# A 20-space weight ring of 8 KiB spaces becomes one of 16 KiB spaces: gate and up of an expert in one transfer

## The chip, the cores and the metric

The kernel runs on 1 core of one Trainium2 chip. The metric is the device time of one execution in microseconds (us); lower is better. Before the change it is 892.16 us, the median of three runs (891.83 to 892.23).

The program feeds the engines by DMAs that SyncE issues: each has 128 rows, one for each partition of the on-chip memory, and the profile counts one packet for each row, and one of a few bytes for each of the 16 DMA engines when a transfer ends.

## What is computed

One decoder block over 256 tokens of width 1024, in float32: a projection of x, dilated attention and a gated linear recurrence side by side, their merge and a layer norm, then a mixture of experts, and a last layer norm. The part that the change touches is the mixture:

```python
s = sigmoid(h @ w_router)                      # 256 tokens, 64 experts
idx, g = top 8 experts of a token, out of its best 4 groups; g normalised, times 2.5
for each expert e and the tokens routed to it:
    a = silu(xb @ w_gate[e]) * (xb @ w_up[e])  # 1024 -> 256
    out = (a @ w_down[e]) * g                  # 256 -> 1024, added to the tokens
y_moe = sum of those + shared_expert(h)
x = layer_norm(alpha * x1 + y_moe + sigmoid(x1 @ ple_gate) * (p @ ple_proj))
```

Each expert has 3 MiB of weights: gate and up with 2 MiB, down with 1 MiB; all 64 are read, 192 MiB.

## The kernel before

**The ring.** Nearly all weights pass through spaces of [128, 2048] float32, that is 8 KiB in each partition and 1 MiB in all. `slot()` (line 71) hands them out in turn from the deque `free`: it takes the first entry, puts it behind the last, and asks the pool of that entry for a tile. The pools are `ring_a` with 9 spaces from the start (line 92), `ring_b` with 6 after the attention and recurrence buffers are closed (line 434), the two spaces of `xhi` and `xlo` (line 478), the one of `x1` (line 875), and two of `ring_c` (line 1020): 18 spaces up to the third unit of experts, then 20. A load into a space waits on SyncE until every reader of its former tile is done, and SyncE issues its loads one after the other, so a waiting load holds up all behind it. Loads with `ordered` keep the order of the program. A pool hands out whichever of its spaces comes free first.

**The experts.** Experts are ranked by their number of tokens (experts 0 to 7 stand in front, `FIXED`) and done in 13 units of two passes (line 816): ten units of pairs (a pass is 2 experts of 64 token places) and three of quads (4 experts of 32 places), in the order P P Q P P P P Q P P P P Q. For a pass, `expert_weights` (line 835) takes three spaces for each expert and loads in the order: first half of gate and up of each expert (k tiles 0 to 3), second half of each (k tiles 4 to 7), down of each. The last unit loads each piece in two transfers of 512 KiB. Where rank, not number, names the expert, SyncE reads the expert's number from a register (`expert_at`).

On TensorE a pass is: `gate_up` over k tiles 0 to 3 for all its experts (`g<-raw,xe`, 3.5 us), the same over k tiles 4 to 7 (3.5 us), transposes, the down product (`g<-raw,hT`, 3.6 us), and the scatter back to the tokens (`acc`). The order of TensorE from the router on is that of the program (`PE_FIXED`).

**The third unit** (line 985, `q == LATE_AT`) is a quad unit with more in it. Its loads in order: 12 spaces of quad pass 1 (experts ranked 40 to 43), `pleg2` and `pleg3` (`late_embedding`, line 884, 1 MiB each), 12 spaces of quad pass 2 (44 to 47), `shgu0`, `shgu1` and `shd` of the shared expert (`late_shared`, line 893), one space `keep` without a load. Then the pairs ranked 8 and 9, 10 and 11, and so on follow.

**Who follows whom in the ring, before.** With 18 spaces, a load takes the space of the 18th before it. So the first halves of quad pass 1 follow the first and second halves of experts 2 and 3; its second halves follow the downs of 2 and 3 and the first halves of 4 and 5; its downs follow the second halves and downs of 4 and 5. `pleg2` and `pleg3` follow the first halves of experts 6 and 7. Quad pass 2 follows, in its order, the second halves and downs of 6 and 7, the first halves of quad pass 1, and four second halves of quad pass 1. The shared weights follow downs of quad pass 1.

Of the kernel before, what the change touches and what calls it, by code (L numbers as in the profile page):

```python
# [11 lines left out]
F32 = mybir.dt.float32  # L12
F32R = mybir.dt.float32r
# [5 lines left out]
S = 256  # L19
D = 1024  # L20
KT = D // 128
AH = 8
NE = 64
# [10 lines left out]
FIXED, SMALL, SMALL_AT = 8, 24, (2, 7, 12)  # L34
# [2 lines left out]
GS_POOL = (0, 2)  # L37
LATE_AT = 2
X_MUL, Q0 = 1, 1
X_AT, C_AT = None, (None, -1)  # L40
# [15 lines left out]
def tile_block(ctx: ExitStack, tc: tile.TileContext, a, out: bass.AP):  # L56
    nc = tc.nc
# [3 lines left out]
    const = ctx.enter_context(tc.tile_pool(name="const", bufs=1))  # L61
    free = deque()

    def add_slots(pl, n, at=None):
        for _ in range(n):
            free.insert(len(free) if at is None else at, (pl, n))

    def add_ring(n, side, name, at=None):
        add_slots(ctx.enter_context(tc.tile_pool(name=name, bufs=1, side=side, reuse_waits="tile")), n, at)

    def slot(dt=F32):

        pl, n = free[0]
        free.rotate(-1)
        return pl.tile([128, 2048], dt, name="raw", tag="raw", bufs=n)

    loads = []

    def load(dst, src, ordered=False):
        ins = nc.sync.dma_start(dst, src)  # L80
        loads.append(ins)
        if ordered:
            tc.keep_in_program_order(ins)
# [5 lines left out]
            load(t[:, c], src[:, c], ordered)  # L89
        return t  # L90

    add_ring(RING_A, "left", "ring_a")
    px0 = ctx.enter_context(tc.tile_pool(name="ringx", bufs=1))

    fixed = {"pe": False}
# [23 lines left out]
    def pieces(src, n, *engine):  # L119
# [311 lines left out]
    phg.close()  # L431
    ph.close()
    pvs.close()
    add_ring(RING_B, "right", "ring_b")


    px = ctx.enter_context(tc.tile_pool(name="px", bufs=1, side="right", reuse_waits="tile"))
# [51 lines left out]
    for i in range(2):  # L489
        for f in range(2):  # L490
            c = slice(512 * f, 512 * f + 512)
# [338 lines left out]
    def expert_at(r):  # L830

        with tc.issue_after(loads[-1].ins):
            return nc.values_load(ids[0:1, r:r + 1], engines=(mybir.EngineType.SP,), min_val=0, max_val=3 * (NE - 1))

    def expert_weights(r0, ne, last=False):

        w = [[] for _ in range(ne)]
        at = [expert_at(r0 + e) if r0 >= FIXED else None for e in range(ne)]
        for n in range(3):
            for e in range(ne):  # L840
                w[e].append(slot())
            parts = 2 if last else 1
            for part in range(parts):
                c = slice(2048 * part // parts, 2048 * (part + 1) // parts)
                for e in range(ne):
                    if at[e] is None:
                        load(w[e][n][:, c], a["exp"][3 * (r0 + e) + n][:, c])
                    else:
                        load(w[e][n][:, None, c], a["exp"][bass.ds(at[e] + n, 1)].rearrange("o p f -> p o f")[:, :, c], True)
        return w  # L850

    def gate_up(gu, kts, xe, off, w):
# [19 lines left out]
    gu0 = bank("g")  # L872
    with tc.issue_after(placed.ins):
        embed(0, gates0, emb0, x1)
    add_slots(pxx, 1, X_AT)
    into = add_emb(0, emb0, True)
    for n in range(2):
        gate_up(gu0, (2 * n, 2 * n + 1), xe, 0, w0)
# [14 lines left out]
    def late_shared():  # L893
        gu = [(raw(a["shgu"][n], ordered=True), 4) for n in range(2)]
        dn = raw(a["shd"], ordered=True)
        keep = slot(F32R)
        hs = ptg.tile([128, 2, 256], F32, name="hs", tag="tg0", bufs=2)
        hth, htl = keep[:, 0:512], keep[:, 512:1024]
        for _ in dense(gu, lambda i, ps: swiglu(hs[:, i], ps), [bank("g") for _ in range(2)]):
            pass  # L900
        hT = bank("t", (128, 2, S))
        for i in range(2):
            for ft in range(2):
                transpose(hT[:, ft, 128 * i:128 * i + 128], hs[:, i, 128 * ft:128 * ft + 128])
        hT = hT.rearrange("p f t -> p (f t)")
        act.activation(hth, hT, CP)
        dve.tensor_sub(htl, hT, hth.bitcast(F32))
        for f in range(2):
            for ft in range(2):
                n = 2 * f + ft  # L910
                whi, wlo = halves()
                act.activation(whi, dn[:, 512 * n:512 * n + 512], CP)
                dve.tensor_sub(wlo, dn[:, 512 * n:512 * n + 512], whi.bitcast(F32))
                for i in range(2):
                    c = slice(256 * ft + 128 * i, 256 * ft + 128 * i + 128)
                    for l, r in ((hth, whi), (htl, whi), (hth, wlo)):
                        mm(acc[i][f], l[:, c], r, start=False, stop=False)
# [67 lines left out]
    for q, (r0, ne) in enumerate(units):  # L985
        if q + 1 < len(units):
            nxt, xnxt, steps = unit(q + 1)
            fill = ((none, steps, steps, none),) * 2
            if q < LATE_AT:
                fill = (none, none if q else into, none if q else into, none), (none, steps, steps, steps)  # L990
            elif q == LATE_AT:
                fill = (none,) * 4, (steps,) * 4
        else:
            rows, lw = slot()[:4, :512], slot().rearrange("p (n d) -> p n d", n=2)
            for n, v in enumerate(("ln2w", "ln2b")):
                load(rows[2 * n:2 * n + 2], a[v].rearrange("(r f) -> r f", r=2), True)
            fill = (norm_weights(rows, lw),) * 4, (none,) * 4
        for pr in range(2):
            r = r0 + ne * pr
            last = q + 1 == len(units) and pr == 1  # L1000
            w = expert_weights(r, ne, q + 1 == len(units)) if r else w0

            def add(i, f, l, halves, first=not r, last=last):
                for n, r in enumerate(halves):
                    mm(acc[i][f], l, r, start=first and f == 1 and n == 0, stop=last and n == 1)
                if last:
                    dve.bn_stats(stats[:, i, f], acc[i][f])

            rest = experts(p2, bank, xe, 128 * pr, s, lambda i: gates2[:, i, r:r + ne], w, add, rest, fill[pr],
                           None if r else gu0)  # L1010
            if q == LATE_AT:
                for _ in rest:
                    pass
                rest = late_embedding() if pr == 0 else late_shared() or ()
            if q == LATE_AT and pr == 0:
                homes = deque(["tg1", "tg1", "xs", "xs", "tg0", "tg0"])
        if q == LATE_AT:
            bd.close()
            for n in range(RING_C):
                add_ring(1, "left", f"ring_c{n}", C_AT[n])  # L1020
        for _ in steps:
            pass
        s, xe = nxt, xnxt
# [42 lines left out]
    pair_no = px.tile([128, 1], F32, name="pair_no")  # L1066
    with tc.If(nr > 1):
        kept = slot()
        total = [[kept[:, 1024 * i + 512 * f:1024 * i + 512 * f + 512] for f in range(2)] for i in range(2)]
        for i in range(2):  # L1070
            for f in range(2):
# [3 lines left out]
        with tc.For_i(1, nr, 1):  # L1075
            dve.tensor_scalar(posm, posm, -float(SLOTS), None, op0=OP.add)
            dve.memset(pair_no, 0.0)
            with tc.For_i(0, NE, 2) as c0:
                with tc.tile_pool(name="po", bufs=1) as po, \
# [5 lines left out]
                    for e in range(2):  # L1085
                        w.append([])
                        at = nc.values_load(ids[0:1, bass.ds(c0 + e, 1)], engines=(mybir.EngineType.SP,),
                                            min_val=0, max_val=3 * (NE - 1))
                        for n in range(3):
                            t = slot()  # L1090
                            nc.sync.dma_start(t[:, None, :], a["exp"][bass.ds(at + n, 1)].rearrange("o p f -> p o f"))
                            w[e].append(t)
# [43 lines left out]
def constants():  # L1136
# [6 lines left out]
    c[:NE, C_COL + 1] = 3 * e  # L1143
# [13 lines left out]
def layouts(i):  # L1157
# [47 lines left out]
    e = np.empty((NE, 3, 128, 2048), np.float32)  # L1205
    gu = e[:, :2].reshape(NE, 2, 128, 4, 2, 256)
    for n, k in enumerate(("expert_w_gate", "expert_w_up")):
        gu[:, :, :, :, n] = g[k][0].reshape(NE, 2, 4, 128, 256).transpose(0, 1, 3, 2, 4)
    e[:, :2] = gu.reshape(NE, 2, 128, 2048)
    e[:, 2] = g["expert_w_down"][0].reshape(NE, 2, 128, 2, 512).transpose(0, 2, 3, 1, 4).reshape(NE, 128, 2048)  # L1210
    r["exp"] = e.reshape(NE * 3, 128, 2048)
    r.update(constants())
    return r

# [17 lines left out]
```

## Time and profile before

| | us |
|---|---|
| median of three runs | 892.16 (891.83 to 892.23) |
| the profiled execution | 890.42 |
| its span in the trace | 888.3 |
| TensorE busy in it | 853.6 (96%) |
| SyncE's DMA queue, share of 16 engines over the span | 76.3% |

Rows of the trace are in microseconds from the start of the span. In groups of instructions, `raw` is a space of the ring, `in_exp_dram` the experts' weights in HBM, `in_pleg_dram` the weights of `pleg2` and `pleg3`, `in_shd_dram` the shared expert's down weights. SPq is SyncE's sequencer, PE is TensorE's matmuls, PEld its weight loads.

### The profile page before, as it was taken

What the parts mean: (1) busy time and instruction counts of PE and PEld (TensorE: products, weight loads), DVE (VectorE), ACT (ScalarE), POOL (GpSimd) and SP (SyncE); (2) the same over time, 40 slices, a digit from 0 to 9 for tenths busy, and PEclk for the clock granted to TensorE, in tenths of its full rate; (3) what the DMA queues carried; (4) which work ended last, traced back from release to release, by engine and by line L of the source; (5) the groups of instructions that cost most, each with busy time, mean ns of one, the idle gap of its engine ahead of it and who ended that gap; (6) DMA issues with size and microseconds to landing.
All of it is one profiled execution on the core that took longest, in us unless ns stands there. A gap on an engine that the chain in (4) does not pass through costs nothing.

```text
span 888.3 us, 13995 instructions
## 1 busy us (share of the span) xinstructions
PE 853.6 (96%) x5200; PEld 563.5 (63%) x5200; DVE 380.1 (43%) x821; ACT 327.0 (37%) x650; POOL 152.0 (17%) x207
## 2 busy tenths in 40 slices
PE   8999999999999999999999989999999999999983
PEld 7899897888879999874444665454544445454220
DVE  6555555695976665773122541122221212222105
ACT  6444544567675545542112341122221212222101
POOL 1015463743300000201210000110210111020001
PEclk9999999999999999989999999999999999999997
DMA  9963424444234887447999999999999999999991
GB/s 339 420 235 127 143 96 142 148 136 144 95 124 160 347 330 308 145 156 272 380 383 401 420 420 421 420 421 421 420 422 417 421 419 422 420 421 403 410 403 63
DMA packets 43776, 270.85 MB, mean 305 GB/s; under 512 B 5252, under 2 KB 5380, under 8 KB 15544
## 3 DMA queue, kind: packets, MB, share of 16 engines
q1 hardware_dynamic: 43352, 269.20, 76.3%
q8 instruction: 42, 0.69, 0.3%
q10 hardware_dynamic: 288, 0.52, 0.2%
q0 software_dynamic: 64, 0.20, 0.1%
q14 instruction: 30, 0.25, 0.1%
HBM read 268.85 MB, written 1.05 MB: 304 GB/s over the span
## 4 chain that ended last, share of the span: by engine, by line
PE 81%; DMA 10%; DVE 6%; issue 1%; ACT 1%; SPq 1%; DVEq 0%; ACTq 0%
PE g L102 30%; PE pj L102 26%; DMA raw<-in_exp_dram 9%; PE t L102 7%; PE acc L102 5%; PE ah L102 4%; PE mix L472 2%; PE sc L102 2%; PE yp L102 1%; PE ap L379 1%; PE t L105 1%; PE pt L258 1%; DMA raw<-in_win_dram 1%; DVE hr L363 1%; PE op L102 1%
## 5 line engine op out<-in xcount | busy, mean ns | idle before, releaser
L102 PE MATMUL g<-raw,xe 128*64 128x512 f32 (+1 forms) x1024 | 196.1, 596 | 3.1 <-DMA raw<-in_exp_dram 2.3
L115 ACT ACTIVATE wh<-raw 128x512 fp32r<-128x512 f32 x213 | 132.2, 630 | 121.3 <-PE pj L102 88.3
L116 DVE TENSOR_TENSOR wl<-raw,wh 128x512 fp32r<-128x512 f32 x184 | 129.4, 715 | 91.1 <-ACT wh L115 70.5
L102 PEld LDWEIGHTS g<-raw,xe 128*64 128x64 f32 (+1 forms) x1024 | 56.8, 126 | 125.7 <-issue 109.5
L102 PE MATMUL pj<-xhi,wh 128*128 128x256 f32 x448 | 128.8, 288 | 0.2 <-DVE hq L364 0.2
L102 PE MATMUL pj<-xlo,wh 128*128 128x256 f32 x448 | 128.2, 286 | 0.0
L102 PE MATMUL pj<-xhi,wl 128*128 128x256 f32 x448 | 128.0, 286 | 0.0
L828 DVE TENSOR_TENSOR h<-h,g 128x256 f32<-128x256 f32 x52 | 21.9, 421 | 200.0 <-ACT h L826 199.1
L790 POOL TENSOR_SCALAR sel<-cst,posm 128x64 fp32r<-128x64 f32 (+1 forms) x120 | 46.4, 419 | 342.3 <-PE t L102 332.1
L102 PE MATMUL g<-raw,hT 128*64 128x512 f32 (+1 forms) x512 | 101.4, 598 | 2.6 <-DVE hT L950 1.6
L102 PEld LDWEIGHTS pj<-xhi,wh 128*128 128x128 f32 x448 | 85.5, 191 | 3.5 <-issue 1.9
L102 PEld LDWEIGHTS pj<-xhi,wl 128*128 128x128 f32 x448 | 85.5, 191 | 3.1 <-issue 2.7
L961 DVE SCALAR_TENSOR_TENSOR yl<-g,gsl,yh 128x512 fp32r<-128x512 f32 x52 | 39.0, 750 | 112.8 <-ACT yh L960 112.8
L102 PEld LDWEIGHTS pj<-xlo,wh 128*128 128x128 f32 x448 | 85.5, 191 | 2.7 <-issue 2.4
L826 ACT ACTIVATE h<-g 128x256 f32<-128x256 f32 x26 | 10.0, 385 | 193.0 <-PE g L102 193.0
L116 POOL TENSOR_TENSOR wl<-raw,wh 128x512 fp32r<-128x512 f32 x29 | 38.5, 1335 | 156.8 <-ACT wh L115 139.8
L960 ACT ACTIVATE yh<-g,gsl 128x512 fp32r<-128x512 f32 x52 | 35.8, 688 | 79.0 <-PE g L102 79.0
L102 PEld LDWEIGHTS g<-raw,hT 128*64 128x64 f32 (+1 forms) x512 | 27.5, 126 | 58.2 <-issue 45.2
L102 PE MATMUL t<-sel,xh 128*128 128x256 f32 x208 | 56.2, 303 | 1.1 <-DVE gsl L942 0.6
L102 PEld LDWEIGHTS t<-sel,xh 128*128 128x128 f32 x208 | 39.1, 188 | 23.1 <-issue 21.5
L804 ACT ACTIVATE xe<-t 128x512 f32<-128x512 f32 x52 | 31.1, 598 | 61.3 <-PE t L102 61.3
L102 PE MATMUL t<-sel,xl 128*128 128x256 f32 x208 | 51.6, 281 | 0.0
(285 smaller groups left out, 1289.1 us busy)
## 6 DMA issues: line engine op xcount, KB each, us to landing
raw<-in_exp_dram SPq DMA_DIRECT2D x168, 1024.0 KB, 15.0
raw<-in_win_dram SPq DMA_DIRECT2D x40, 1024.0 KB, 5.4
raw<-in_exp_dram SPq DMA_DIRECT2D x48, 512.0 KB, 10.2
raw<-in_wab_dram SPq DMA_DIRECT2D x8, 768.0 KB, 4.5
raw<-in_wo_dram SPq DMA_DIRECT2D x4, 1024.0 KB, 4.8
raw<-in_pleg_dram SPq DMA_DIRECT2D x4, 1024.0 KB, 6.9
raw<-in_win_dram SPq DMA_DIRECT2D x8, 256.0 KB, 5.9
raw<-in_shgu_dram SPq DMA_DIRECT2D x2, 1024.0 KB, 17.6
```

What stands on the lines that cost most here:

```text
L102: pinned(pe.matmul(o, l, r, start=start, stop=stop))
L105: pinned(pe.transpose(o, t, ident))
L115: act.activation(hi, src, CP)
L116: (lo_engine or dve).tensor_sub(lo, src, hi.bitcast(F32))
L258: pe.transpose(pt[:, b], pr[:, 128 * b:128 * b + 128], ident)
L472: ins = pe.matmul(mix[i][f], l[:, ts], r[f], start=j == n == 0, stop=j == 7 and n == 2)
L790: by.tensor_scalar(s[:, i, w * e:w * e + w], iota[:, 0:w], pos_of(i)[:, e:e + 1], None, op0=OP.is_equal)
L804: act.activation(xe[k2], ps, CP)
L826: act.activation(h, ps[:, 0:256], AF.Sigmoid)
L828: dve.tensor_mul(h, h, ps[:, 256 * n:256 * n + 256])
L960: act.activation(yh, y, CP, scale=gsl)
L961: dve.scalar_tensor_tensor(yl, y, gsl, yh.bitcast(F32), op0=OP.mult, op1=OP.subtract)
```

## The change

A space is now [128, 4096] float32 (16 KiB in a partition, 2 MiB), called wide, with a few single ones of 8 KiB. Sizes are (wide, single): `ring_a` (4, 1), `ring_b` (3, 0), `ring_c` (1, 0), `xhl` one wide, `x1` one single; 8 wide and 2 single up to the third unit, then 9 and 2, in bytes the same as before. A whole wide is given back when all its readers are done. `wide()` takes the first wide entry of the deque. `slot()` takes the first entry of either kind; of a wide one it returns the first half, and the next call of `slot()`, whoever makes it, gets the second half (`second`).

The weights of gate and up of an expert lie in HBM as one row of 16 KiB in each partition (`expgu`), those of down apart (`expd`). For passes ranked 8 and up, but for the last unit, an expert's gate and up come in one transfer of 2 MiB with rows of 16 KiB, where there were two of 1 MiB with rows of 8 KiB. Passes ranked 0 to 7 (four pairs) take two wides for the two halves of both experts and load them in four transfers of 1 MiB. The last unit takes a wide for each expert and loads it in four transfers of 512 KiB in the order it had.

```diff
-RING_A, RING_B, RING_C, RING_X, STOP = 9, 6, 2, 2, ""
+RING_A, RING_B, RING_C, RING_X, STOP = (4, 1), (3, 0), (1, 0), 1, ""
...
+    second = []
+
+    def space(dt, *kinds):
+
+        pl, kind, n = r = next(r for r in free if r[1] in kinds)
+        free.remove(r)
+        free.append(r)
+        return pl.tile([128, 4096 if kind == "wide" else 2048], dt, name=kind, tag=kind, bufs=n), kind
+
+    def wide():
+
+        return space(F32, "wide")[0]
+
+    def slot():
+
+        if second:
+            return second.pop()
+        t, kind = space(F32, "wide", "raw")
+        if kind == "wide":
+            second.append(t[:, 2048:])
+            t = t[:, :2048]
+        return t
...
-    xhi, xlo = (px0.tile([128, 2048], F32R, name=n, tag="raw", bufs=RING_X).rearrange("p (k t) -> p k t", k=KT)
-                for n in ("xhi", "xlo"))
+    xhl = px0.tile([128, 2, KT, S], F32R, name="xhl", tag="wide", bufs=RING_X)
+    xhi, xlo = xhl[:, 0], xhl[:, 1]
...
     def expert_weights(r0, ne, last=False):
...
+        at = [expert_at(r0 + e) if r0 >= FIXED else r0 + e for e in range(ne)]
...
+        whole = not last and r0 >= FIXED
+        gu = [wide() for _ in range(ne)]
+        if r0 < FIXED:
+            w = [[t[:, 2048 * e:2048 * e + 2048] for t in gu] for e in range(ne)]
+        else:
+            w = [[t[:, 2048 * n:2048 * n + 2048] for n in range(2)] for t in gu]
+        if whole:
             for e in range(ne):
-                w[e].append(slot())
...
+                fetch(gu[e], "expgu", e, slice(0, 4096))
+        for n in range(2 if whole else 0, 3):
+            if n == 2:
                 for e in range(ne):
...
+                    w[e].append(slot())
+            for c0 in range(0, 2048, 1024 if last else 2048):
+                c = slice(c0, c0 + (1024 if last else 2048))
+                for e in range(ne):
+                    o = 2048 * n if n < 2 else 0
+                    fetch(w[e][n][:, c], "expgu" if n < 2 else "expd", e, slice(o + c.start, o + c.stop))
...
-        keep = slot(F32R)
+        keep = space(F32R, "raw")[0]
```

The loop for a second round of tokens (from line 1067) is changed alike; it did not run in the profiled execution.

## Rows read from the trace of the kernel before

**Rows 1.** The page: span, and GB/s moved in 40 equal slices of it.

```profile
span 888.3 us, 13995 instructions
...
GB/s 339 420 235 127 143 96 142 148 136 144 95 124 160 347 330 308 145 156 272 380 383 401 420 420 421 420 421 421 420 422 417 421 419 422 420 421 403 410 403 63
```

**Rows 2.** The chain that ended last, near its end: start, us, what.

```profile
783.85 3.35 PE g L102 x15
787.20 19.79 DMA raw<-in_exp_dram
...
858.98 10.53 DMA raw<-in_exp_dram
...
869.54 1.90 PE g L102 x10
```

**Rows 3.** PEld's waits in 787 to 880: us in total, times, longest.

```profile
PEld g L102 <- DMA raw<-in_exp_dram: 21.0, 23, 1.1
```

**Rows 4.** Stretches: us, busy time of each engine (instructions), TensorE clock, DMA share, GB/s.

```profile
455.00:482.00 27.00, 26.15 (x176) 12.42 (x176) 4.93 (x14) 5.19 (x10) 3.32 (x8) 1.00 0.96 385
...
540.00:668.00 128.00, 127.36 (x662) 58.99 (x664) 24.66 (x56) 25.86 (x48) 15.32 (x40) 1.00 1.01 421
668.00:787.00 119.00, 118.69 (x684) 55.74 (x676) 24.24 (x59) 25.17 (x47) 15.23 (x40) 1.00 1.01 420
787.00:868.00 81.00, 77.46 (x374) 26.86 (x372) 13.13 (x33) 13.04 (x24) 0.10 (x1) 1.00 1.00 401
```

**Rows 5.** SyncE's own waits in 425 to 484.

```profile
SPq L80 <- PE g L102: 40.6, 9, 6.2
```

**Rows 6.** SyncE's own waits in 540 to 668.

```profile
SPq L80 <- PE g L102: 86.7, 25, 6.2
```

**Rows 7.** SyncE's own waits in 690 to 787.

```profile
SPq L80 <- DMA raw<-in_exp_dram: 67.3, 38, 2.5
```

**Rows 8.** SyncE's DMA queue in 540 to 668 (rows of 8 KiB): packets, MB, share.

```profile
q1 hardware_dynamic: 7376, 53.73, 101.0%
```

**Rows 9.** SyncE's DMA queue in 830 to 860 (rows of 4 KiB).

```profile
q1 hardware_dynamic: 3368, 12.26, 102.6%
```

**Rows 10.** The page's queue of instruction fetches: packets, MB, share of 16 engines.

```profile
q8 instruction: 42, 0.69, 0.3%
```

**Rows 11.** TensorE in time order: start, us, operation; experts 6 and 7, then quads.

```profile
453.86 7.09 PE L102 MATMUL g<-raw,xe 128*64 128x512 f32 x32
...
464.62 3.65 PE L102 MATMUL g<-raw,hT 128*64 128x512 f32 x16
...
471.23 7.07 PE L102 MATMUL g<-raw,xe 128*32 128x512 f32 x64
...
511.46 3.64 PE L102 MATMUL g<-raw,hT 128*32 128x512 f32 x32
```

**Rows 12.** A load issued to an idle queue, at 397.

```profile
L80 SPq DMA_DIRECT2D raw<-in_exp_dram x1: 328/328/328, 397.3 to 397.3; - x1
...
DMA to landing us min/median/max: 4.7/4.7/4.7
```

**Rows 13.** Issues of pleg2 and pleg3: duration in ns, first and last start.

```profile
L80 SPq DMA_DIRECT2D raw<-in_pleg_dram x2: 338/354/370, 457.5 to 458.0; - x2
...
DMA to landing us min/median/max: 6.9/6.9/6.9
```

**Rows 14.** The two loads issued at 468 (third and fourth expert of quad pass 2).

```profile
L80 SPq DMA_DIRECT2D raw<-in_exp_dram x2: 332/332/332, 468.3 to 468.9; - x2
...
DMA to landing us min/median/max: 7.3/8.3/9.2
```

**Rows 15.** The last shared weight, shd.

```profile
L80 SPq DMA_DIRECT2D raw<-in_shd_dram x1: 328/328/328, 486.5 to 486.5; - x1
...
DMA to landing us min/median/max: 19.9/19.9/19.9
```

More of the change, by code (lines that the diff above doesn't have):

```diff
@@ L62, in tile_block, with add_slots, add_ring @@
     free = deque()
[L64 to L75, printed above, removed]
+    def add_slots(pl, wides, singles=0, at=None):
+        for kind, n in (("wide", wides), ("raw", singles)):
+            for _ in range(n):
+                free.insert(len(free) if at is None else at, (pl, kind, n))
+    def add_ring(wides, singles, side, name, at=None):
+        add_slots(ctx.enter_context(tc.tile_pool(name=name, bufs=1, side=side, reuse_waits="tile")), wides, singles, at)
+    second = []
[14 more added lines that the diff above has]
+        return t
     loads = []
@@ L90, in raw @@
         return t
-    add_ring(RING_A, "left", "ring_a")
+    add_ring(*RING_A, "left", "ring_a")
     px0 = ctx.enter_context(tc.tile_pool(name="ringx", bufs=1))
@@ L433, in tile_block @@
     pvs.close()
-    add_ring(RING_B, "right", "ring_b")
+    add_ring(*RING_B, "right", "ring_b")
     px = ctx.enter_context(tc.tile_pool(name="px", bufs=1, side="right", reuse_waits="tile"))
@@ L832, in expert_at, with fetch @@
         with tc.issue_after(loads[-1].ins):
-            return nc.values_load(ids[0:1, r:r + 1], engines=(mybir.EngineType.SP,), min_val=0, max_val=3 * (NE - 1))
+            return nc.values_load(ids[0:1, r:r + 1], engines=(mybir.EngineType.SP,), min_val=0, max_val=NE - 1)
     def expert_weights(r0, ne, last=False):
-        w = [[] for _ in range(ne)]
-        at = [expert_at(r0 + e) if r0 >= FIXED else None for e in range(ne)]
-        for n in range(3):
+        at = [expert_at(r0 + e) if r0 >= FIXED else r0 + e for e in range(ne)]
+        def fetch(dst, name, e, c):
+            if r0 < FIXED:
+                load(dst, a[name][at[e]][:, c])
+            else:
+                load(dst[:, None], a[name][bass.ds(at[e], 1)].rearrange("o p f -> p o f")[:, :, c], True)
+        whole = not last and r0 >= FIXED
+        gu = [wide() for _ in range(ne)]
+        if r0 < FIXED:
+            w = [[t[:, 2048 * e:2048 * e + 2048] for t in gu] for e in range(ne)]
+        else:
+            w = [[t[:, 2048 * n:2048 * n + 2048] for n in range(2)] for t in gu]
+        if whole:
             for e in range(ne):
-                w[e].append(slot())
-            parts = 2 if last else 1
-            for part in range(parts):
-                c = slice(2048 * part // parts, 2048 * (part + 1) // parts)
+                fetch(gu[e], "expgu", e, slice(0, 4096))
+        for n in range(2 if whole else 0, 3):
+            if n == 2:
                 for e in range(ne):
[L846 to L849, printed above, removed]
+                    w[e].append(slot())
[4 more added lines that the diff above has]
+                    fetch(w[e][n][:, c], "expgu" if n < 2 else "expd", e, slice(o + c.start, o + c.stop))
         return w
@@ L874, in tile_block @@
         embed(0, gates0, emb0, x1)
-    add_slots(pxx, 1, X_AT)
+    add_slots(pxx, 0, 1, X_AT)
     into = add_emb(0, emb0, True)
@@ L1018, in tile_block @@
             bd.close()
-            for n in range(RING_C):
-                add_ring(1, "left", f"ring_c{n}", C_AT[n])
+            add_ring(*RING_C, "left", "ring_c", C_AT)
         for _ in steps:
@@ L1068, in tile_block @@
         kept = slot()
+        second.clear()
         total = [[kept[:, 1024 * i + 512 * f:1024 * i + 512 * f + 512] for f in range(2)] for i in range(2)]
@@ L1087, in tile_block @@
                         at = nc.values_load(ids[0:1, bass.ds(c0 + e, 1)], engines=(mybir.EngineType.SP,),
[L1088 to L1092, printed above, removed]
+                                            min_val=0, max_val=NE - 1)
+                        gu, dn = wide(), slot()
+                        for t, name in ((gu, "expgu"), (dn, "expd")):
+                            nc.sync.dma_start(t[:, None, :], a[name][bass.ds(at, 1)].rearrange("o p f -> p o f"))
+                        w[e] += [gu[:, :2048], gu[:, 2048:], dn]
                     mine = po.tile([128, 2, NE], F32, name="mine")
@@ L1142, in constants @@
     c[:NE, C_COL] = -IN_FRONT * np.minimum(e, FIXED) - e
-    c[:NE, C_COL + 1] = 3 * e
+    c[:NE, C_COL + 1] = e
     t = np.arange(S).reshape(128, 2).T.reshape(S)
@@ L1204, in layouts @@
     r["shd"] = np.ascontiguousarray(g["shared_w_down"][0].reshape(2, 128, 2, 512).transpose(1, 2, 0, 3)).reshape(128, 2048)
[L1205 to L1211, printed above, removed]
+    gu = np.stack([g[k][0].reshape(NE, KT, 128, 256) for k in ("expert_w_gate", "expert_w_up")], axis=3)
+    r["expgu"] = np.ascontiguousarray(gu.transpose(0, 2, 1, 3, 4)).reshape(NE, 128, 4096)
+    r["expd"] = np.ascontiguousarray(
+        g["expert_w_down"][0].reshape(NE, 2, 128, 2, 512).transpose(0, 2, 3, 1, 4)).reshape(NE, 128, 2048)
     r.update(constants())
```

2 lines of the change are left out of this document (1 added, 1 removed).

## The prediction, made before the changed kernel was run

> **What bounds the kernel now.** First the GB/s by slices [rows 1]: from about 480 us to 800 us the DMA engines move some 420 GB/s without a break, and the stretches give 421 and 420 GB/s at a DMA share of 1.01 [rows 4]. In the same stretches TensorE is busy 127.36 of 128 us and 118.69 of 119 us, so both look like the bound. The chain of waits decides: TensorE's last step before 787 is followed by nothing but expert transfers up to 869.5, and only 19 us of work come after them [rows 2]. The list of TensorE's weight loads agrees: all 21.0 us that they wait for expert weights lie behind 787 [rows 3]. So TensorE runs ahead of need until 787 and then starves: the end is set by when the unbroken stream of weights began, its bytes and its rate. A us lost by the stream anywhere after it became unbroken is a us of time; a us lost by TensorE before 787 is not, as long as it frees spaces in time.
>
> When does the stream become unbroken? In 455 to 482 it moves only 385 GB/s [rows 4]: there SyncE waits for spaces that TensorE still reads, 40.6 us in nine waits [rows 5]. In 540 to 668 SyncE waits for spaces too (86.7 us, [rows 6]), but with several transfers queued behind one another, so the engines never run dry. In 690 to 787 it waits for earlier transfers to land, 2.5 us each [rows 7], which is a full queue. So the third unit, at 455 to 515, is where a change of the ring is paid for, and shd, the last shared weight, is my marker: issued at 486.5, landed 19.9 later, at 506.4 [rows 15].
>
> **The change part by part: the rate.** Rows of 8 KiB go at 53.73 MB in 128 us [rows 8], 2.498 us for 1 MiB; rows of 4 KiB at 12.26 MB in 30 us [rows 9], 1.283 us for half of that, 2.566 for 1 MiB. Half as many packets for the same bytes save 0.068 us. If the cost is one of packets, the next halving saves half of it, 0.034 us for 1 MiB, and a 2 MiB transfer takes 4.93 instead of 5.00 us. 16 KiB rows of weights are not in the trace, so both ends: no saving at all (a row costs what two cost) is the low one; the high one is that nothing but bytes counts, from the same two rows 2 × 0.068 = 0.136 us for 2 MiB. The only packets of 16 KiB in the trace are instruction fetches: 0.3% of 16 × 888.3 us over 42 packets is 1.0 us each [rows 10], against 0.31 us for 8 KiB (128 × 16 × 1.01 us over the 6,558 that are not end marks, 7376 × 8/9; [rows 8]); they end in an instruction buffer and not in the weights' spaces, so I give that no more than a word: were it so for weights, 40 transfers would lose 40 × 8 × 0.4 = some 120 us. I take 0.07 us, the row-by-row fit. Transfers of the new kind behind shd: 32 experts in pairs and 8 in quads, 40; saving 2.8 us (0 to 5.4).
>
> The Trainium skill, DMA: Bandwidth & Descriptors, section Where 436 GB/s comes from, has a ceiling of 435.2 GB/s for 16 engines; the trace's 421 lies 3% under it. By that ceiling 2 MiB would take an estimated 4.82 us, and the 40 transfers would save 7.2 us.
>
> **The ring.** Bytes are equal, so what counts is who shares a wide. I walk the deque with the new `slot()`. Experts 4 and 5: two wides for the halves, down of 4 in the single of `ring_a`, down of 5 in the first half of a wide of `ring_a`; its second half stays in `second`. Experts 6 and 7: two wides, down of 6 takes that left half, down of 7 the single of `x1`. So downs of 5 and 6 share a wide, and it is free only after the down product of the pair 6, 7: 464.62 + 3.65 = 468.3 [rows 11]. Quad pass 1 then takes, in turn, the wides of 2 and 3 (two halves, then downs), the two halves of 4 and 5, the single, and for its last down one more wide of `ring_a`, whose other half goes to pleg2; pleg3 takes the next wide of `ring_a`. Two of that pool can serve these two: the first halves of 6 and 7 (free when half of `gate_up` at 453.86 is done, 457.4) and the wide of downs 5 and 6 (468.3). Whichever goes first, pleg3 cannot be issued before 468.3. Before, it went out at 458.0 [rows 13], and four transfers of quad pass 2 were behind it by 468.9 [rows 14].
>
> Now step by step. Down of 43 and pleg2 go at 457.5 and 458.0 and are in by about 465, as they were. pleg3 goes at 468.3 to an idle queue: a transfer alone lands 4.7 us after its issue [rows 12], 2.2 of which are not data, so it lands at 473.0; the engines stood idle from 465 to 470.5. The 2 MiB of expert 44 land at 477.9. Expert 45 needs the wide of expert 40, held for all of `gate_up` of quad pass 1: 471.23 + 7.07 = 478.3 [rows 11] (before, half of such spaces came free after its first 3.5 us). Issued at 478.4, its data start at 480.6, another 2.7 us idle. From there nothing is dry: three experts 14.8 us, four downs 10.0, shgu0, shgu1 and shd 7.5: shd lands at 512.9, against 506.4. That is 6.5 us late. The restarts may be slower than 4.7: the load issued at 468.3 before the change took 7.3 us [rows 14] though what was queued ahead of it explains 6.1. Two restarts at 0 to 1.2 us each; I take 1.4 for both.
>
> Behind shd one more place is tight. The wide of pleg3 has the down of expert 44 in its other half, and expert 9 needs it: free at 511.46 + 3.64 = 515.1 [rows 11]. Expert 8 ends at 517.8; a load issued at 515.1 brings data at 517.3. It fits by half a us; I take 0, bound 0 to 3 (TensorE late by so much through a late weight). From 540 on each wide of gate and up is held up to 3.5 us longer than half of it was, but before the change the stream had several transfers of 2.5 us queued in its slot waits; and being late it has more free spaces, not fewer: 0. Gate and up of both experts must land before the pair can begin where 2 MiB of 4 were enough; TensorE will wait in the quads at about 680 and 700, some 4 us, and gives it back, since it starves behind 787 anyway: 0.
>
> **Small parts.** The first 455 us are bound by TensorE, whose projections find their weights early; pairing spaces there makes a load wait for two readers instead of one, and the queue is mostly empty: 0, ±1 for another order of instructions. SyncE issues 48 transfers fewer (0.33 us each, [rows 14]), but in every stretch read it waits on others [rows 5 to 7]: 0. The halves of the first pairs and of the last unit are read from rows 16 KiB apart instead of 8: no row shows a cost, 0. The tail after the last byte is untouched.
>
> **Sum.** 6.5 late + 1.4 for restarts − 2.8 by the rate = 5.1 us. On the profiled execution's 890.42 (2.1 around its span of 888.3) that is 895.5; the median of the runs lies 1.74 above it, so 897.2, rounded 897.0.
>
> **The rivals.** (a) The stream is not held at 468.3, because the walk errs or a half is given back alone. Then only the rate is left: 48 transfers × 0.07 = 3.4, 888.8 us: faster. For it: the trace says nothing of shared spaces. Against: the walk is plain in the code. It decides if pleg3 goes out before 461. (b) Packets cost nothing beyond bytes: 5.4 instead of 2.8 saved, and restarts at 4.7: 6.5 − 5.4 = 1.1, 893.3 us, no change that shows. The stream's steady 421 in one stretch and 420 in the next [rows 4] is against it. The ceiling of the Trainium skill, DMA: Bandwidth & Descriptors, section Where 436 GB/s comes from, points this way, and no row here reaches it. (c) A row of 16 KiB travels as two packets: nothing saved, 6.5 + 1.4 = 7.9, 900.1 us. (d) Expert 9 misses its half us and a third gap opens at 517: up to 3 more, 900.2 us. (e) A fixed cost of every transfer that halving their number would save: a lone one has 2.2 us beyond its data [rows 12], 48 × 2.2 = 106 us, 787 us. The full queue of [rows 7] hides it: landings come 2.5 us apart. [...]
>
> **How the numbers follow.** Forecast with its own spread (894.0 to 899): 0.52. (c) and (d) together: 0.17. (b): 0.15. (a): 0.14. (e) and other gains: 0.01; a far slower row of 16 KiB: 0.01. This kernel's measurement tells 0.2% from no change, that is 1.8 us: faster is below 890.4, slower above 893.9. Of (b) most is "same"; the forecast's low edge too: faster 0.15, same 0.15, slower 0.70. The range must hold 8 in 10: it takes in (b), the forecast and (c) and (d), and leaves out (a) and the far ends: 891.0 to 902.0.
>
> **What would show it.** In SyncE's waits of the third unit, one of about 10 us on TensorE before pleg3, ending at 468.3; GB/s in 455 to 482 well under 385; shd landing at 512 to 515; in 540 to 780 some 425 GB/s at a DMA share of 1.0. Wrong it is if pleg3 goes out at 461 or earlier, if the rate stays at 421 or passes 430, or if the GB/s has holes behind 520.

## The result

The changed kernel takes 899.53 us (median of four, 897.68 to 901.96), the kernel before 892.0 beside it: a ratio of 1.0085, 95% interval 1.0068 to 1.0101. It is slower, 2.5 us beyond the predicted 897.0: just outside the forecast's own spread (894.0 to 899) and inside the range (891.0 to 902.0). The profiled execution of after took 897.68, with a span of 895.52 against 888.26, 7.26 longer. One execution of r3, below, took 2102.92 us and is not in its ratio.

The page of after, span and GB/s by slices, beside [rows 1]:

```profile
span 895.5 us, 13734 instructions
...
GB/s 333 420 217 94 145 92 157 136 142 160 112 119 95 374 314 341 112 234 261 379 300 353 423 427 424 424 424 426 426 425 421 427 426 424 425 424 410 365 404 83
```

Stretches of after (us, busy time of each engine with its instructions, TensorE clock, DMA share, GB/s), beside [rows 4]:

```profile
455.00:482.00 27.00, 26.66 (x171) 12.64 (x169) 5.26 (x14) 5.36 (x11) 3.33 (x8) 1.00 0.75 272
...
540.00:668.00 128.00, 127.36 (x652) 59.62 (x654) 24.80 (x57) 25.85 (x48) 15.35 (x40) 1.00 1.01 425
668.00:787.00 119.00, 113.85 (x638) 51.57 (x632) 22.21 (x53) 22.62 (x42) 9.99 (x24) 0.99 1.01 425
...
840.00:846.00 6.00, 5.99 (x41) 2.19 (x41) 1.80 (x6) 1.62 (x4) 0.00 (x0) 1.00 0.87 348
846.00:852.00 6.00, 4.83 (x24) 1.39 (x23) 0.75 (x1) 1.28 (x2) 0.00 (x0) 1.00 0.87 288
```

Three things differ from before. In the third unit the stream pauses longer: 272 GB/s where there were 385. In the steady stretches it is faster: 425 instead of 421 and 420. And a new hole stands near the end: 348 and 288 GB/s in 840 to 852, where before moves 410:

```profile
840.00:852.00 12.00, 11.01 (x43) 2.56 (x42) 0.75 (x1) 1.29 (x2) 0.00 (x0) 1.00 1.03 410
```

SyncE's queue of after in 540 to 668 (packets, MB, share), beside [rows 8], shows that a row of 16 KiB is one packet: 4989 packets for 54.36 MB, where 53.73 MB took 7376.

```profile
q1 hardware_dynamic: 4989, 54.36, 100.7%
```

The third unit more closely. The issues of `pleg2` and `pleg3`, of gate and up of expert 45, and of `shd` in after (duration in ns, first and last start, then us to landing), beside [rows 13] and [rows 15]:

```profile
L98 SPq DMA_DIRECT2D wide<-in_pleg_dram x2: 339/800/1262, 459.5 to 469.9; - x2
...
L98 SPq DMA_DIRECT2D wide<-in_expgu_dram x1: 343/343/343, 479.9 to 479.9; - x1
...
DMA to landing us min/median/max: 8.2/8.2/8.2
...
L98 SPq DMA_DIRECT2D raw<-in_shd_dram x1: 328/328/328, 493.0 to 493.0; - x1
...
DMA to landing us min/median/max: 22.9/22.9/22.9
```

`pleg3` was held to 469.9, and expert 45 to 479.9; `shd` landed at 493.0 + 22.9 = 516.0 instead of 506.4.

Both kernels run the same 5,200 matrix products in the same order, so TensorE's lateness can be read product by product: how much later than before it starts the same product. At 472 it is 1.57 us, which arose before 400 us (r11, below). Taking it off, `shd` is 7.95 late. The last expert load ahead of the last norm's weights lands 296.89 us behind `shd`, against 300.54 before: 3.65 regained. From there to the end of the span it takes 82.66 against 81.28, some 1.4 more. 1.57 + 7.95 − 3.65 + 1.39 = 7.26, the whole difference. The four terms follow one another in time, so they must add up to it; what makes each of them is for the experiments to show.

The chain that ended last, near its end (start, us, what), beside [rows 2], and SyncE's own wait in 830 to 850:

```profile
814.68 7.02 PE g L120 x32
842.26 3.67 PE g L120 x32
847.99 7.53 DMA wide<-in_expgu_dram
855.54 10.23 DMA wide<-in_expgu_dram
865.78 11.36 DMA wide<-in_expd_dram
...
SPq L98 <- PE g L120: 4.9, 1, 4.9
```

The stream still ends the chain, but it has a link in it that before had not: SyncE waits 4.9 us for the down product at 842.26. The wide for the last expert's gate and up follows the one of the downs of experts 56 and 57.

### The profile page after: what moved, and what is told of

Same layout as the page of the kernel before. It is cut to its first block, busy times and chain, and to the rows that moved or that the text cites. A ratio compares the mean times of both kernels' runs of the same rounds, so it can differ in the third digit from the quotient of the medians.

```text
span 895.5 us, 13734 instructions
## 1 busy us (share of the span) xinstructions
PE 851.8 (95%) x5200; PEld 562.3 (63%) x5200; DVE 377.1 (42%) x821; ACT 326.6 (36%) x650; POOL 152.6 (17%) x207
## 4 chain that ended last, share of the span: by engine, by line
PE 82%; DMA 8%; DVE 6%; issue 2%; ACT 1%; SPq 1%; DVEq 0%; ACTq 0%
PE g L120 32%; PE pj L120 25%; PE t L120 7%; PE acc L120 6%; DMA wide<-in_expgu_dram 5%; PE ah L120 4%; PE mix L490 2%; PE sc L120 2%; DMA wide<-in_expd_dram 1%; PE t L123 1%; PE ap L397 1%; PE yp L120 1%; DMA lbl<-in_lbt_dram 1%; DMA wide<-in_xt_dram 1%; PE pt L276 1%
## 5 line engine op out<-in xcount | busy, mean ns | idle before, releaser
L120 PE MATMUL g<-wide,xe 128*64 128x512 f32 (+1 forms) x1024 | 197.9, 599 | 9.1 <-DMA wide<-in_expgu_dram 8.4
L120 PE MATMUL pj<-xhl,wh 128*128 128x256 f32 x896 | 169.8, 287 | 1.8 <-DVE hq L382 1.8
L133 ACT ACTIVATE wh<-wide 128x512 fp32r<-128x512 f32 x194 | 120.5, 630 | 111.4 <-PE pj L120 80.8
L134 DVE TENSOR_TENSOR wl<-wide,wh 128x512 fp32r<-128x512 f32 x167 | 117.3, 714 | 85.1 <-ACT wh L133 68.0
L120 PEld LDWEIGHTS pj<-xhl,wh 128*128 128x128 f32 x896 | 140.4, 191 | 7.8 <-issue 3.9
L120 PEld LDWEIGHTS g<-wide,xe 128*64 128x64 f32 (+1 forms) x1024 | 57.3, 127 | 133.2 <-issue 110.7
L120 PE MATMUL pj<-xhl,wl 128*128 128x256 f32 x448 | 128.0, 286 | 0.0
L120 PEld LDWEIGHTS pj<-xhl,wl 128*128 128x128 f32 x448 | 85.5, 191 | 3.1 <-issue 2.7
L120 PE MATMUL g<-wide,hT 128*64 128x512 f32 (+1 forms) x384 | 84.2, 598 | 2.9 <-DMA wide<-in_expd_dram 1.8
L120 PE MATMUL pj<-wh,xhl 128*128 128x512 f32 x224 | 69.9, 398 | 3.0 <-ACT wh L133 2.5
L120 PEld LDWEIGHTS g<-wide,hT 128*64 128x64 f32 (+1 forms) x384 | 22.9, 126 | 46.5 <-issue 36.2
```

Of the source, the lines that this page charges most:

```text
L120: pinned(pe.matmul(o, l, r, start=start, stop=stop))
L133: act.activation(hi, src, CP)
L134: (lo_engine or dve).tensor_sub(lo, src, hi.bitcast(F32))
```

## The experiments

Every run below is compared with the kernel before on the same chip (medians 892.1 to 892.6). "Lateness" is that of TensorE at 472; "`shd` net" is the landing of `shd` less that lateness; "last net" the landing of the last expert load ahead of the last norm's weights, less the lateness at 650. All are in us, from the issue and landing times of one profiled execution of each kernel. In the edits, `...` stands for lines left out.

| kernel | ratio to before, 95% interval | lateness | `shd` net | last net |
|---|---|---|---|---|
| before | 1 | 0 | 506.4 | 807.0 |
| after, first profile | 1.0085 (1.0068, 1.0101) | 1.6 | 514.4 | 811.3 |
| r0 after again | 1.0086 (1.0072, 1.0099) | 4.1 | 514.6 | 811.3 |
| r1 two transfers of 8-KiB rows | 1.0118 (1.0102, 1.0134) | 5.3 | 514.5 | 814.4 |
| r2 one transfer of 8-KiB rows | 1.0142 (1.0124, 1.0160) | 4.4 | 515.0 | 814.8 |
| r3 last unit by halves | 1.0057 (1.0042, 1.0072) | 2.8 | 514.4 | 811.0 |
| r4 own wides | 1.0119 (1.0100, 1.0138) | 1.5 | 514.4 | 814.5 |
| r5 before, pleg3 later | 1.0003 (0.9993, 1.0013) | 0.5 | 506.9 | 808.1 |
| r6 own wides, last by halves | 1.0102 (1.0085, 1.0118) | 4.9 | 514.5 | 814.0 |
| r7 the same, lbl on GpSimd's queue | 1.0113 (1.0096, 1.0130) | 6.2 | 514.6 | 814.3 |
| r8 downs first | 1.0067 (1.0051, 1.0083) | 1.6 | 509.5 | 810.9 |
| r9 quad by halves | 1.0028 (1.0015, 1.0040) | 5.0 | 511.0 | 808.1 |
| r10 both | 1.0045 (1.0027, 1.0063) | 4.3 | 506.9 | 809.0 |
| r11 both, lbl early | 1.0023 (1.0015, 1.0032) | −0.2 | 507.2 | 809.3 |

**r0, the changed kernel again**, no edit.

> The changed kernel as it is, beside its variants on one chip. Theory: 7.2 us longer than the kernel before = 1.5 from the first 455 us, 8 from the hold of pleg3 and of expert 45 in the third unit, minus 3.65 from 16-KiB rows, 1.8 from a hole at 840 to 852, minus 0.4 at the very end. Expected 899.5 us within 1.8, ratio 1.0085 within 0.002.

It came out as expected, 1.0086. The net columns agree with the first profile to 0.2 us though the two executions are 3.3 us apart: 2.6 of what differs between them is the early lateness.

**r1 and r2, what the rate comes from.** r1 loads the same wide in two transfers:

```diff
-                fetch(gu[e], "expgu", e, slice(0, 4096))
+                for c in (0, 2048):
+                    fetch(gu[e][:, c:c + 2048], "expgu", e, slice(c, c + 2048))
```

> Changed kernel, but gate and up of a whole expert come in two transfers of 1 MiB with rows of 8 KiB, into the same wide in the same order. Theory that the rows give the rate: GB/s in 540 to 787 back to 420 or 421, 40 transfers x 0.09 = 3.65 us of gain lost, so 903 us, 1.2% above the kernel before; shd unchanged within 1 us. Rival that the rate comes from something else in the new ring (who waits when): still 425 GB/s and 899.5 us.

r2 keeps one transfer of 2 MiB, out of two blocks of rows of 8 KiB:

```diff
...
+            elif c.stop - c.start == 4096:
+                load(dst.rearrange("p (n f) -> p n f", n=2),
+                     a["expgu"][bass.ds(2 * at[e], 2)].rearrange("n p f -> p n f"), True)
...
```

> Changed kernel, but gate and up lie in memory as two halves with rows of 8 KiB, and one transfer of 2 MiB fetches both, 256 rows of 8 KiB. Theory that the size of a row gives the rate: 420 or 421 GB/s in 540 to 787, 903 us. Rival that the number of transfers gives it (half as many issues and ends): 425 GB/s, 899.5 us. Between them each has a share.

The stretch 540 to 668 of r1, then of r2:

```profile
540.00:668.00 128.00, 127.36 (x636) 61.30 (x634) 24.96 (x57) 26.41 (x49) 15.27 (x40) 0.99 1.01 421
```

```profile
540.00:668.00 128.00, 127.36 (x637) 60.98 (x636) 25.20 (x57) 26.26 (x49) 15.35 (x40) 0.99 1.01 421
```

Both are back at 421 GB/s. From `shd` to the last load it takes 300.2 us in r1 and 299.9 in r2, against 296.9 in after and 300.5 before. So rows of 16 KiB are worth 3.0 to 3.3 us, and half as many transfers 0.3 at most; the last 0.3 to before is there without long rows. Neighbouring loads on the full queue agree: 2 MiB land 4.90 us behind the load ahead of them in after, 4.97 in r2, and 1 MiB 2.49 before. By the ratios r1 loses 2.9 us against r0, r2 5.0; their profiled spans are 902.0 and 902.3, and I read no difference between them out of intervals that overlap.

**r3, the hole at 840.** The last unit takes its spaces by `slot()` in the order of loading:

```diff
+            if last and n < 2:
+                for e in range(ne):
+                    w[e].append(slot())
...
```

> Changed kernel, but the last unit takes its spaces for gate and up half by half in the order of loading, as before the change, so no expert's whole wide stands behind the down weights of experts 56 and 57. Theory that this wait makes the hole at 840 to 852: GB/s there back from 348 and 288 to some 405, time 1.8 us less, 897.7 us. Rival: the hole only moves to the downs of the last pass, because the stream's spaces all come free with that down product: within 0.5 us of 899.5.

The stretches 840 to 846 and 846 to 852 of r3:

```profile
840.00:846.00 6.00, 5.99 (x36) 2.49 (x36) 1.89 (x7) 1.85 (x4) 0.00 (x0) 1.00 1.03 409
846.00:852.00 6.00, 6.00 (x43) 1.98 (x36) 1.50 (x2) 1.97 (x3) 0.00 (x0) 1.00 1.03 409
```

The hole is gone, and by the ratios 2.6 us with it (1.8 expected). That whole wides in the last unit make it is shown; that it is the last expert's, behind the downs of 56 and 57, rests on the wait of 4.9 us above.

**r4, the shared wide of downs 5 and 6.**

```diff
+                if r0 == 4:
+                    t = wide()
+                    w[0].append(t[:, :2048])
+                    w[1].append(t[:, 2048:])
                 for e in range(ne):
-                    w[e].append(slot())
+                    if r0 == 6:
+                        w[e].append(space(F32, "raw")[0])
+                    elif r0 != 4:
+                        w[e].append(slot())
...
```

The lines left out give the last norm's weights a wide of `ring_a`.

> Changed kernel, but downs of experts 4 and 5 share one wide and downs of 6 and 7 take the two single spaces, so no wide waits for the pair 6, 7 in the third unit; the last norm's weights take a wide of ring_a as they do in the changed kernel. Theory that the shared wide of downs 5 and 6 costs some 8 us: pleg3 is issued within 2 us of pleg2, 455 to 482 moves over 370 GB/s, shd lands within 2 us of where the early part puts it (506.4 plus that lateness), time 8 us less, 892 us. Rival that whole wides held by experts 40 and 45 are the larger part: pleg3 early, but shd still 3 to 5 us late, 895 to 897 us. Rival that TensorE's own lateness in the quads holds the end: within 1 us of 900.

My first theory, 8 us for the shared wide, fell here. `pleg3` went out at 459.5, right behind `pleg2`; `shd` net stayed at 514.4. SyncE's wait in 455 to 484 of after, then of r4 (us in total, times, longest):

```profile
SPq L98 <- PE g L120: 19.6, 3, 9.1
```

```profile
SPq L98 <- PE g L120: 20.3, 2, 16.6
```

And the stretches 465 to 470, 470 to 474 and 474 to 482, of after and of r4:

```profile
465.00:470.00 5.00, 5.00 (x29) 2.31 (x28) 1.18 (x2) 1.31 (x3) 2.48 (x7) 1.00 0.26 107
470.00:474.00 4.00, 4.00 (x32) 2.90 (x35) 0.75 (x1) 1.85 (x3) 0.00 (x0) 1.00 0.75 262
474.00:482.00 8.00, 7.66 (x66) 2.83 (x58) 1.43 (x6) 0.77 (x2) 0.00 (x0) 1.00 0.88 304
```

```profile
465.00:470.00 5.00, 5.00 (x28) 2.34 (x27) 1.18 (x2) 1.39 (x3) 2.42 (x6) 1.00 1.04 437
470.00:474.00 4.00, 4.00 (x32) 2.84 (x35) 0.75 (x1) 1.78 (x3) 0.00 (x0) 1.00 0.62 266
474.00:482.00 8.00, 7.66 (x66) 2.83 (x58) 1.43 (x6) 0.77 (x2) 0.00 (x0) 1.00 0.16 39
```

The pause did not go, it moved: 107 GB/s at 465 became 437, and 304 at 474 became 39. One wait of 16.6 us stands where two stood: expert 45 needs the whole wide of expert 40, and that is read until 479.8 whatever happens before. The ratio is worse than r0's: from `shd` to the last load it takes 299.8 us, 2.9 more. The edit also shifts who shares a wide later, and the trace shows where that costs: less the lateness at 650, r4's landings are 0.3 us behind those of after at 618 and 3.8 behind at 652, and a wide that after loads at 601.1 is loaded at 616.6. r8 to r10 avoid it.

**r5, pleg3 later in the old ring.**

```diff
+        w = [raw(a["pleg"][2], ordered=True)]
+        ahead = [slot() for _ in range(3)]
+        w.append(raw(a["pleg"][3], ordered=True))
+        held.extend(ahead)
...
```

> Kernel before, old ring of 8-KiB spaces, but the space of pleg3 is handed out three places later, so it is the one of the down of expert 6; order of loads as before. Theory that the hold alone stops the stream: pleg3 issued at 468.3 plus the early lateness, some 5.5 us idle less up to 2.3 that stood idle in 455 to 482 anyway, shd 3.2 to 5.5 us late, 897 us (895.6 to 898). Rival that the stream has slack there: shd within 1 us, 892.4 us.

Inconclusive. A pool hands out the space that is free first, so `pleg3` got one at 461.5 and not at 468.3; that delay, 3.0 us beyond the lateness, cost `shd` 0.5 and the time nothing that shows.

**r6 and r7.** r6 joins the edits of r3 and r4. r7 adds:

```diff
-    load(lbl, a["lbt"])
+    nc.gpsimd.dma_start(lbl, a["lbt"])
```

and the same for `gain`.

> Changed kernel with both edits: downs of 4 and 5 in one wide and of 6 and 7 in singles, and the last unit's spaces taken half by half. If the two losses stand side by side, 8 and 2.6 us less than the changed kernel's 900.0: 889.4 us, some 3 us faster than the kernel before, which is what 16-KiB rows are worth alone. If other late wides take their place behind 515, above 892.

> As the one with both edits, and the two small loads of the recurrence (lbl, gain) go out on GpSimd's queue, so that they don't stand behind two weight transfers at 166. Theory that this wait makes TensorE 1.6 us late at 181 and 3.2 where its clock falls behind the pause: lateness against the kernel before in 200 to 370 is 1 us instead of 2.7 to 4.8, of which 1.15 comes back at 370 to 392 anyway: 0.5 to 2 us less than with both edits, 887.4 to 888.9 us. Rival that the time in front of 455 is given back in the third unit: as with both edits, within 0.5 us.

Both missed. r6 is r4 without the hole at 840: `shd` net 514.5 as before. In r7 the small load is issued on GpSimd at 169.9, takes 5.7 us and lands at 175.6, no sooner than in after (175.4): it took 2.4 us less than the 8.1 on SyncE's queue, but went out 2.6 us later (167.3 in after).

**r8, r9, r10: two waits one behind the other.** The new theory is that the third unit loses its 8 us to whole wides that come free late, with single spaces idle beside them, and that `pleg3`'s wait only hides in that. All three have the edits of r3 and r4, with the later sharing mended (the wide of `shd` is not shared and the two single spaces stay next to each other in the deque). r8 loads the downs of 44 and 45 ahead of gate and up of 45:

```diff
+                if r0 == 44 and e == 1:
+                    for k in range(ne):
+                        w[k].append(slot())
+                    for k in range(2):
+                        fetch(w[k][2], "expd", k, slice(0, 2048))
...
```

r9 puts experts 40 to 43 into their wides half by half, in eight transfers of 1 MiB:

```diff
-        whole = not last and r0 >= FIXED
+        whole = not last and r0 >= FIXED and r0 != 40
...
+        elif r0 == 40:
+            w = [[gu[2 * n + e // 2][:, 2048 * (e % 2):2048 * (e % 2) + 2048] for n in range(2)] for e in range(ne)]
...
```

r10 does both.

> New theory: two waits stand one behind the other in the third unit, pleg3's (to 469.9) and that of expert 45 for the whole wide of expert 40 (to 479.8); the second hides the first, so that taking away the first alone brought shd nothing (514.4 less the early lateness, with or without it). Here the first is gone (own wides), the last unit goes by halves, the wide of shd isn't shared, and the downs of 44 and 45, whose single spaces are free at 468.3, are loaded ahead of gate and up of 45. They fill some 5 us of the pause at 474 to 482: shd, less the early lateness, at 509.5 to 511, 892.5 us. The theory of a shared wide alone expects no change of shd: 514.4, 897 us.

> Own wides, last unit by halves, shd's wide not shared; order of the downs as in the changed kernel; but experts 40 to 43 lie in their wides half by half (first halves of 40 and 41 in one, of 42 and 43 in another, the second halves likewise, in 8 transfers of 1 MiB), so that two wides come free after the first half of gate_up, 3.5 us sooner. New theory: gate and up of 45 issued at 474.9 plus the early lateness instead of 478.4, shd less the early lateness at 510.5 to 511, 893 us. The theory of a shared wide alone: shd 514.4, 897 us.

> Both: downs of 44 and 45 first, and experts 40 to 43 by halves. If late release of whole wides and idle single spaces are the whole of the loss in the third unit, the pause is gone: 455 to 482 moves 370 GB/s or more, shd less the early lateness at 506.4 to 507.5, 7 us less than the changed kernel with the last unit by halves (896.9): 889.5 us, some 2.5 us faster than the kernel before, what rows of 16 KiB are worth. If another wait follows, shd stays behind 509 and the time above 891.

The stretch 455 to 482 of r8, of r9, of r10:

```profile
455.00:482.00 27.00, 26.66 (x171) 12.69 (x169) 5.26 (x14) 5.38 (x11) 3.31 (x8) 1.00 0.88 343
```

```profile
455.00:482.00 27.00, 27.00 (x168) 12.57 (x168) 4.58 (x9) 5.79 (x10) 3.31 (x8) 1.00 0.81 318
```

```profile
455.00:482.00 27.00, 27.00 (x172) 12.42 (x168) 4.58 (x9) 5.80 (x10) 3.33 (x8) 1.00 0.98 399
```

`shd` net came as expected in all three: 509.5 (509.5 to 511), 511.0 (510.5 to 511), 506.9 (506.4 to 507.5). The loss of the third unit is explained to 0.4 us, with `pleg3`'s wait gone in all three: no run shortens the second wait and keeps the first, so what the first would then cost is not shown. The times were not as expected: r8 898.1 instead of 892.5, r9 895.9 instead of 893, r10 896.5 instead of 889.5. The last column says that it went behind `shd`: r10 is 7.5 us ahead of after there, and 2.3 at the last load. The stretch 655 to 665 of before, after and r10:

```profile
655.00:665.00 10.00, 10.00 (x62) 5.47 (x62) 3.08 (x7) 3.23 (x6) 3.33 (x8) 1.00 1.01 421
```

```profile
655.00:665.00 10.00, 10.00 (x56) 5.34 (x53) 2.33 (x6) 2.93 (x6) 3.33 (x8) 1.00 1.03 429
```

```profile
655.00:665.00 10.00, 10.00 (x56) 5.27 (x54) 1.58 (x5) 1.86 (x4) 3.23 (x8) 1.00 0.87 332
```

Here the loads of the second quad unit's second pass wait for wides. In after its first is issued at 657.2 with three transfers queued ahead of it, in r10 at 660.1 with one. Less the lateness at 650 both are 655.7, and the pass's other loads of gate and up agree as well: the third goes out at 663.0 and the fourth at 671.1 in after, r8, r9, r10 and r11, so it is TensorE that sets them. r10's stream is still 4.9 us ahead of after when it gets there (less the lateness, its last landing before the pass is at 657.2, that of after at 662.1); it runs dry, and its fourth load lands 2.3 ahead. The other 2.6 were lost on the way there. The pass's fourth load in r10, its issue and us to landing:

```profile
L98 SPq DMA_DIRECT2D wide<-in_expgu_dram x1: 333/333/333, 675.6 to 675.6; - x1
...
DMA to landing us min/median/max: 8.3/8.3/8.3
```

8.3 us is what expert 45 needed on a nearly idle queue (8.2, above); after's loads of 600 to 690 have a median of 20.9. The kernel before passes here at 421 GB/s, with spaces half as large that come free sooner. r9, which was given only 3.4 us, keeps 3.2 of them, while r8 keeps 0.4 of 4.9. Half of that difference arises at the pass's fourth load, which lands, less the lateness, at 681.7 in after, 681.3 in r8, 680.1 in r9 and 679.4 in r10. The other half arises at the four downs behind it, which take 9.9 us in r9 and 11.5 in the other three. Why they differ is open.

**r11, the early lateness.** As r10, with

```diff
             load(dist, a["dist"])
+            lbl = pv.tile([128, 2, AH], F32, name="lbl")
+            load(lbl, a["lbt"])
```

and `gain` likewise.

> As the one before, and the two small loads of the recurrence (lbl, gain) are issued by SyncE right behind dist, near 20 us, into a buffer that lives from the start, instead of at 167 behind two transfers of weights. TensorE's pause near 181 (1.6 us, and as much again where its clock falls behind it) goes: lateness in 200 to 370 like that at 26, 1 to 2 us; 1.15 of it came back at 370 to 392 anyway: 888 us, 0.5 to 2 us less than without this. Rival: the stream's start in the third unit doesn't hang on TensorE's early lateness: no difference.

The stretch 182 to 192 of after, of r0, of r11, and the wait of VectorE for `lbl` in 165 to 185 of after:

```profile
182.00:192.00 10.00, 9.09 (x58) 6.69 (x59) 6.94 (x14) 4.95 (x13) 3.67 (x3) 1.00 0.73 279
```

```profile
182.00:192.00 10.00, 9.50 (x52) 7.54 (x52) 6.72 (x14) 5.05 (x12) 3.19 (x3) 0.83 0.75 273
```

```profile
182.00:192.00 10.00, 10.00 (x65) 7.03 (x65) 8.22 (x14) 6.16 (x16) 3.85 (x4) 1.00 0.86 303
```

```profile
DVE lm L324 <- DMA lbl<-in_lbt_dram: 1.6, 1, 1.6
```

The lateness of after has three parts: 1.1 us by 12 us, 1.6 more at 179 to 180, and 1.15 that come back at 375 to 380. With `lbl` loaded at 12 us, the middle step is gone: the lateness of 200 to 370 is 1.1 us (2.7 in the first profile of after, 3.8 in r0). The other two parts are not the ring's: r5, with the old ring, is 1.5 late by 12 us and gets 1.15 back. What comes back is time that the profiled execution of before had lost itself, at a lower clock. The stretch 374 to 382 of before, then of after:

```profile
374.00:382.00 8.00, 6.91 (x42) 6.48 (x43) 6.11 (x10) 2.54 (x5) 0.00 (x0) 0.79 0.56 207
```

```profile
374.00:382.00 8.00, 5.98 (x47) 5.11 (x45) 7.93 (x27) 4.58 (x10) 0.00 (x0) 1.00 0.16 36
```

The time of r11 is 2.0 us less than r10's by the ratios, at the edge of what was expected, out of intervals that just overlap. No kernel with the new ring beats the one before; r11 comes nearest, 0.15 to 0.32% above it.

## Why the prediction came near, step by step

- **The bound.** Right in the main. TensorE lost 9.1 us in the second quad unit, from 1.55 late at 678 to 10.6 at 717, at twice the 4 us I had, and that is no term of the sum: the chain still ends with the stream. That a us lost by the stream anywhere behind 480 is a us of time holds less far than I wrote: of the 7.5 us that r10 gained at `shd`, 2.3 were left at the last load. [rows 7] was also misread: 67.3 us in 38 waits are 1.8 us on the mean, and 2.5 the longest.
- **The third unit: the size near, the cause half seen, and luck in the sum.** 6.5 + 1.4 = 7.9 was predicted, 8.0 came. `pleg3` was held to 468.3 plus the lateness, as walked, and expert 45 until TensorE had read expert 40. But in the working itself the landing of `shd` at 512.9 is counted from the issue of expert 45 at 478.4, so `pleg3` has no part in it as long as it and expert 44 are in by then. I did not see that: I took the hold of `pleg3` for what decides, as rival (a) and the sign of being wrong show ("pleg3 goes out at 461 or earlier"). In r4 it went out at 459.5 and nothing was saved. The price is that of wides released whole, 3.5 us later than halves, and of two singles that no load could use until the downs' turn (r8, r9, r10). The 1.4 for two restarts agreed by luck: the first has no effect on `shd`; expert 45 took 8.2 us to land where the working has 2.2 + 4.9 = 7.1, and the loads behind it took 27.9 instead of 27.4.
- **The rate.** Right in mechanism and size: 0.07 us for each transfer of 2 MiB was predicted, and landings 4.90 instead of 4.97 us apart are that; 2.8 us in all against the 3.0 to 3.3 of r1 and r2. The 3.65 regained behind `shd` hold some 0.3 more, whose cause is not shown. (The 6,558 packets of the working should be 6,556; nothing hangs on it.) Rivals (b), (c) and (e) fall: something is saved, but not down to bytes alone, and a row stays one packet. The Trainium skill, DMA: Bandwidth & Descriptors, section Where 436 GB/s comes from, gives a ceiling of 435.2; 425 GB/s is 2.3% under it, and no run is above 425 in 540 to 668 or in 668 to 787.
- **Expert 9.** It fitted, as taken: it landed 5.0 us behind expert 8, a full queue's spacing, and no gap stands at 517. Rival (d) did not happen.
- **"Being late it has more free spaces: 0."** Right, and r10 shows it from the other side: a stream that comes 4.9 us sooner to the second quad unit's second pass meets wides that are not free.
- **The early part, 0 ± 1.** Mis-sized. In after two transfers of weights go out 0.4 us apart at 166, as the two halves of one wide would, and `lbl` behind them is there at 175.4 instead of 170.5. That made 1.6 us, in r0 3.2; r11 shows that it was the load. The other two parts of the lateness, 1.1 and −1.15, cancel by chance. r0 loses another 1.4 us at 392 to 397, where short products of 0.28 us in before take 0.42 in r0 (mean clock of 386 to 406: 0.91 and 0.83): again the execution and not the ring.
- **The last unit, 0.** Failed. I looked at row addresses there and not at who follows whom: the last expert's wide waits for the downs of 56 and 57. Between 1.4 (the sum above) and 2.6 us (r3). By the prediction's own signs this counts against it: it said that it is wrong if the GB/s has holes behind 520.

The two misses, 1.6 and 1.4, less the 0.85 that came back beyond the predicted 2.8, are 2.1 of the 2.2 us between the predicted 5.1 and the 7.26 of the profile; the last 0.05 are the third unit's. The median came out at 899.53, near what rivals (c) and (d) would have given (900.1 and 900.2), though neither happened: a number alone would not have told them apart.

## What to carry to other kernels

When a ring's spaces are made larger, cost them by when a whole space comes free: here each wide was released 3.5 us later than its first half had been, and that ate more than twice what longer rows gave (8.0 against 3.0 to 3.3 us). Two waits in line do not add up: before pricing the first, ask when the second would have ended anyway. And a stream that is made earlier gains only up to the next space that the reader sets free; look for that place before counting the gain.

## What the hardware showed that I had not expected

- The rate of a full queue rises with the row: with two thirds of the bytes in rows of 16 KiB it is 425 GB/s, with rows of 8 KiB alone 421 (before, r1, r2). Whether one transfer or two carry the 2 MiB makes 0.3 us in 300.
- A transfer of 2 MiB on an idle queue landed 8.2 us after its issue, 3.3 beyond its 4.9 of data (expert 45 in r4); one of 1 MiB took 4.7, 2.2 beyond its 2.5 [rows 12].
- A pause of TensorE of about 1.6 us near 180 cost as much again in some executions: r0 shows a mean granted clock of 0.83 in 182 to 192, so part of it at 1.2 GHz, and is 3.2 us later behind it; the first profile of after, with the same pause and a clock of 1.00 there, is 1.6 later. Two executions can differ so without any edit: before has a clock of 0.79 in 374 to 382 and after 1.00, which is worth 1.15 us.
- A small load moved from SyncE's queue to GpSimd's landed no sooner: 5.7 us instead of 8.1 from its issue, but issued at 169.9 instead of 167.3 (r7).
